# A decoder trunk on one core: the sparse-attention indexer summed pair by pair, and four loads moved between queues

## The chip, the cores and the metric

The kernel runs on one core of a Trainium2 chip. It is one launch; all weights are read from HBM once. The metric is the device time of that launch in microseconds (us). Times of single instructions and waits come from one profiled execution, whose own time stands beside the other runs below.

## What is computed

Two decoder layers on 512 tokens of width 1024, all in float32. Layer 0 mixes tokens with a gated linear recurrence (HGRN2), layer 1 with a sparse attention (DSA); each is followed by a SwiGLU feed-forward block with a causal convolution of width 3. Before each of the four blocks, and at the end, stands an RMS norm. The part that the change touches most is the indexer of layer 1, cut here to its core:

```python
proj = rms_norm(h, attn_norm[1]) @ w_in
q, k, v, q_idx, k_idx, w_idx = split(proj)      # q_idx: 8 heads of 64; k_idx: 64; w_idx: 8
dots   = einsum('bthd,bsd->bths', q_idx, k_idx)
scores = einsum('bths,bth->bts', relu(dots), w_idx * (8 ** -0.5 * 64 ** -0.5))
scores = where(key_pos <= q_pos, scores, -1e30)
sel    = top_k(scores, 128)                     # the keys that this query attends to
```

Attention then runs over the selected keys alone, here as a dense product with a mask: a key that was not selected gets a large penalty.

## The kernel before, in words

**Layout and engines.** Activations lie transposed, 128 features on the partitions by 512 tokens, in 8 blocks. Every float32 operand of a large product is split into a high and a low part (fp32r), and a product is three matmuls: high by high, high by low, low by high (`mm3`, L169 to L171). A weight tile of 128 x 1024 is loaded by `wunit` (L150, on SP's queue), and split on ACT (`whi`, L143) and on DVE or GpSimd (`wlo`, L144). Where `lo_engine` is None, `wlo` is made by ACT (L158) and an accumulating DMA of GpSimd's queue (L160), and `whi` by ACT at L159. There are three buffers of `whi` and of `wlo`: a new tile waits until the projection that read the buffer is finished. `proj_T` is one such projection: 24 matmuls into one PSUM bank `pj`.

**What sets the order.** TensorE's order is the program's own: `weave` runs a main generator and, by costs that each yields, lets side generators (`add_side`) put their matmuls between. The other engines' order is set by a scheduler when the kernel is built, and each runs its instructions in that order. So a matmul that stands early in TensorE's order and whose operand comes late holds up everything behind it.

**The third norm.** The sum of squares of layer 1's input (`sqa`, L215) goes through TensorE (`pq`, L240), DVE, and GpSimd (`rstd_c`, L248, four columns), and is turned back into rows by four transposes (`pr`, L252) and an ACT copy (`rstd_r`, L253). `norm_chain(wait)` yields `wait` before `pq`, and 4.2 before `pr`.

**The indexer.** `head_in` projects `k_idx` and `w_idx` first (72 columns, called pk here), then the eight heads of `q_idx` as four blocks of two heads, called b0 to b3. Of each block `stack` makes `qh` and `ql`: ACT copies the upper rows to `qh` (L675) and the lower to `ql` (L676), then DVE subtracts the residues into the other halves (L677, L678). `kw_evac` and `kw_weights` make `ki_h`, `ki_l` and the head weights `wN`. After all four blocks `dots` runs: for each of the query tiles t = 1, 2, 3 and for each block the two heads' products (`pi`, L749, widths 256, 384, 512), ReLU on ACT (L759, two buffers `relu`), and the weighted sum into `sc[t]` on DVE (L755, L760). Meanwhile TensorE goes on with the projections of K, V and q (`rest_in`), whose results DVE scales (`tmp`, L696).

**The selection.** `top` finds the 128 largest scores by 16 rounds of MAX (L774) and MATCH_REPLACE (L776) on DVE, first for t = 1 alone, then for t = 2 and 3 together, and writes the mask `sel` (L779). The attention units take `sel1` and later `sel2` and `sel3` as an operand of TensorE (L860), so TensorE waits there if DVE is late.

**Start.** The first instructions load `cols` (all norm gains and small vectors, 25 KB, ACT's queue), the conv constants `convc` (L117, ACT's queue), the first half of x in pieces (L413) and the first weights (L150), both on SP's queue. The first real matmul (L425) needs `whi` (L141), and x scaled by `cols` (L133).

Of the kernel before, what the change touches and what calls it, by code (L numbers as in the profile page):

```python
# [8 lines left out]
F32 = mybir.dt.float32  # L9
# [3 lines left out]
AF = mybir.ActivationFunctionType  # L13
ALU = mybir.AluOpType
# [3 lines left out]
P = 128  # L18
D = 1024
T = 512  # L20
# [3 lines left out]
NEG = -1e30  # L24
# [24 lines left out]
def trunk(ctx: ExitStack, tc: tile.TileContext, xT, vecs, convs, hgrn_w_in, hgrn_w_out, dsa_w_in, dsa_w_out,  # L49
          rel_bias, ffn_w_up, ffn_w_down, c_masks, c_onehot, out, dbg=None, stop=99):  # L50
    nc = tc.nc
# [9 lines left out]
    def bank(name):  # L61
        return ps.tile([P, 512], F32, name=name, tag="bank")
# [16 lines left out]
    nrm = ctx.enter_context(tc.tile_pool(name="nrm", bufs=2))  # L79

    cols = const.tile([P, 49], F32, name="cols")
    nc.scalar.dma_start(cols, vecs)
    gn_col = cols[:, 48:49]
    ident = const.tile([P, P], F32, name="ident")
    make_identity(nc, ident)
    convc = const.tile([P, 2, 4, 2 * FB], F32, name="convc")
# [12 lines left out]
    rstd_c = const.tile([P, TT], F32, name="rstd_c")  # L99
# [9 lines left out]
    def late_constants():  # L109
        yield 6.0  # L110
        raw = wraw.tile([P, 1024], F32, name="wr", tag="wr")
        mk = raw[:, :len(LEVELS) * P + 192]
        nc.scalar.dma_start(mk, c_masks)
        nc.vector.tensor_copy(masks, mk[:, 192:].rearrange("p (l t) -> p l t", t=P))
        for i in range(3):
            nc.vector.tensor_copy(pairs[:, i], mk[:, None, i * 64:i * 64 + 64].to_broadcast([P, TT, 64]))
        nc.scalar.dma_start(convc.rearrange("p l w b -> p (l w b)"), convs)  # L117
        nc.scalar.dma_start(far, bass.AP(tensor=rel_bias.tensor, offset=rel_bias.offset + (REL_BUCKETS - 1) * AH,
                                         ap=[[0, P], [1, AH]]))
        rb, oneh = raw[:REL_BUCKETS, 1000:1000 + AH], raw[:REL_BUCKETS, 576:576 + BAND]  # L120
        nc.scalar.dma_start(rb, rel_bias)
        nc.scalar.dma_start(oneh, c_onehot)
        yield 6.0
        pz = bank("pz")
        nc.tensor.matmul(pz[:AH, :BAND], rb, oneh, start=True, stop=True)
        bz = mk[:AH, :BAND]
        nc.vector.memset(bz, -NEG)
        nc.scalar.activation(bz[:, 127:383], pz[:AH, :256][:, ::-1], AF.Copy, scale=-1.0)
        nc.scalar.dma_start(Z, bz)
# [16 lines left out]
    def wunit(src, nk, n, first=False, dst=None):  # L146

        raw = wraw.tile([P, 1024], F32, name="wr", tag="wr")
        rv = raw[:, :nk * n].rearrange("p (k n) -> p k n", k=nk)
        nc.sync.dma_start(rv, src.rearrange("(k p) n -> p k n", p=P))  # L150
        if dst:
            hi, lo = (a.rearrange("p a b -> p (a b)") for a in dst)
        else:
            hi = wsp.tile([P, 1024], F32R, name="whi", tag="whi")
            lo = wsp.tile([P, 1024], F32R, name="wlo", tag="wlo")
        if lo_engine[0] is None and not dst:

            nc.scalar.activation(lo[:, :nk * n], raw[:, :nk * n], AF.Copy, scale=-1.0)  # L158
            nc.scalar.activation(hi[:, :nk * n], raw[:, :nk * n], AF.Copy)  # L159
            nc.gpsimd.dma_start(lo[:, :nk * n].rearrange("p (k n) -> p k n", k=nk),  # L160
                                src.rearrange("(k p) n -> p k n", p=P), accum_op=ALU.add)
        else:
            split(hi[:, :nk * n], lo[:, :nk * n], raw[:, :nk * n], lo_engine[0] or nc.vector,
                  nc.vector if first else None)
        return (hi[:, :nk * n].rearrange("p (k n) -> p k n", k=nk),
                lo[:, :nk * n].rearrange("p (k n) -> p k n", k=nk))
# [18 lines left out]
    side, done = [], set()  # L185

    def add_side(gen, rate=1.0):
        side.append([gen, rate, 0.0])
# [472 lines left out]
    with ExitStack() as sx:  # L661
        ds_ = sx.enter_context(tc.tile_pool(name="ds", bufs=1))
        bias = ds_.tile([P, AH, T], F32, name="bias")
        qh = ds_.tile([P, KB, T], F32R, name="qh")
        ql = ds_.tile([P, KB, T], F32R, name="ql")
# [5 lines left out]
        def stack(b, src, lo):  # L671

            a, c = qh[:, b, :], ql[:, b, :]
            top_, bot = rows2
            nc.scalar.activation(a[top_], src[top_], AF.Copy)  # L675
            nc.scalar.activation(c[bot], src[bot], AF.Copy)  # L676
            lo.tensor_tensor(a[bot], src[top_], a[top_].bitcast(F32), op=ALU.subtract)  # L677
            lo.tensor_tensor(c[top_], src[bot], c[bot].bitcast(F32), op=ALU.subtract)  # L678
# [4 lines left out]
        wN = ds_.tile([P, TT, 8], F32, name="wN")  # L683
        scs = ds_.tile([P, 9 * P], F32, name="scs")
        sc = [None, scs[:, 7 * P:], scs[:, 4 * P:7 * P], scs[:, :4 * P]]
        m8 = ds_.tile([P, TT, 8], F32, name="m8")

        with ExitStack() as sy:
            iy = sx.enter_context(tc.tile_pool(name="iy", bufs=1))
            ix = sy.enter_context(tc.tile_pool(name="ix", bufs=1))  # L690
            ki_h = ix.tile([P, T], F32R, name="ki_h")
            ki_l = ix.tile([P, T], F32R, name="ki_l")
# [16 lines left out]
            def kw_weights():  # L709
                tmp = kw.pop()  # L710
                pw = bank("pw")
                for t in range(TT):
                    nc.tensor.transpose(pw[:, t * 72:(t + 1) * 72], tmp[:72, t * P:(t + 1) * P], ident[:72, :72])
                for t in range(TT):
                    nc.vector.tensor_scalar(wN[:, t, :], pw[:, t * 72 + 64:(t + 1) * 72], 8 ** -0.5 * 64 ** -0.5,
                                            rstd_c[:, t:t + 1], op0=ALU.mult, op1=ALU.mult)

            def setup():

# [13 lines left out]
            def head_in():  # L733
                pk = yield from proj_T(w_in, O_KI, 72)
                for b in range(4):
                    o = yield from proj_T(w_in, O_QI + b * P,
                                          hook=({7: lambda: kw_evac(pk)}, {2: kw_weights}, None, None)[b])
                    lo_engine[0] = nc.gpsimd
                    stack(4 + b, o, nc.vector)

            def dots():
                for t in range(1, TT):
                    w = (t + 1) * P
                    ts_ = slice(t * P, (t + 1) * P)
                    for b in range(4):
                        o = [bank("pi") for _ in range(2)]
                        for k_ in (ki_h, ki_l):
                            for e in range(2):
                                nc.tensor.matmul(o[e][:, :w], (qh, ql)[e][:, 4 + b, ts_], k_[:, :w],  # L749
                                                 start=k_ is ki_h, stop=k_ is ki_l)  # L750
                        yield 0.22 * (t + 1)
                        for e in range(2):
                            i = 2 * b + e
                            if i == 0:
                                nc.vector.tensor_scalar(sc[t], o[e][:, :w], 0.0, wN[:, t, 0:1],  # L755
                                                        op0=ALU.max, op1=ALU.mult)
                            else:
                                r_ = ix.tile([P, T], F32, name="relu", bufs=2)
                                nc.scalar.activation(r_[:, :w], o[e][:, :w], AF.Relu)  # L759
                                nc.vector.scalar_tensor_tensor(sc[t], r_[:, :w], wN[:, t, i:i + 1], sc[t],  # L760
                                                               op0=ALU.mult, op1=ALU.add)
                    nc.gpsimd.affine_select(sc[t][:, w - P:], sc[t][:, w - P:], pattern=[[-1, P]], base=0,
                                            channel_multiplier=1, compare_op=ALU.is_ge, fill=NEG)
                    done.add(f"sc{t}")
                    if t == 1:
                        add_side(top((1,)), 0.4)

            def top(ts):

                while any(f"sc{t}" not in done for t in ts):  # L770
                    yield 0.5
                for r in range(16):
                    for t in ts:
                        nc.vector.max(m8[:, t, :], sc[t])  # L774
                    for t in ts:
                        nc.vector.match_replace(sc[t], m8[:, t, :], sc[t], -3e38)  # L776
                    yield sum(2 * (0.065 + (t + 1) * P / 960) for t in ts)
                for t in ts:
                    nc.vector.tensor_scalar(sel[t], sc[t], -2e38, -NEG, op0=ALU.is_gt, op1=ALU.mult)  # L779
                    done.add(f"sel{t}")  # L780
                if 3 not in ts:
                    add_side(top((2, 3)), 0.55)
# [26 lines left out]
                    done.add(f"q{b}")  # L809
                done.add("q8")  # L810

            add_side(norm_chain())
            add_side(setup())
            weave(head_in())
            add_side(dots(), 1.0)
            rest = rest_in()
            for c in rest:
                weave([c])
# [220 lines left out]
```

## Time and profile before

| | |
|---|---|
| three runs | 1273.42, 1273.68 (median), 1275.24 us |
| profiled execution: its own time | 1276.48 us |
| profiled execution: span of its instructions | 1274.7 us |
| busy in the span: TensorE (PE) | 1251.4 us (98%) |
| busy in the span: VectorE (DVE) | 803.0 us (63%) |
| busy in the span: ScalarE (ACT) | 599.6 us (47%) |
| busy in the span: GpSimd (POOL) | 138.8 us (11%) |
| DMA | 124.05 MB, mean 97 GB/s |

TensorE is busy almost throughout; the time outside the span is 1.8 us. The profiled execution is 2.8 us above the median of the three others. A busy PE counts a matmul from its start to a modelled end, so two that follow each other overlap; steps from start to start tell the pace.

### The profile page before, as it was taken

The numbers are of one execution on the slowest core, as the hardware profiler recorded it, in microseconds if no ns is written. First come the engines' busy times: TensorE is split into PE (matmuls) and PEld (weight loads), VectorE is DVE, ScalarE is ACT, GpSimd is POOL, SyncE is SP. The second block draws the span as 40 slices with busy tenths as digits, with TensorE's granted clock in tenths as the row PEclk, the third lists the DMA queues.
The fourth block names the chain that finished last, engine by engine and source line by source line (L and its number), as shares of the span: only waits on it lengthen the run. The fifth ranks groups of instructions, "written<-read, shape, count | busy, mean of one in ns | idle before, by whom it ended". The sixth has DMA issues, their size and how long they took to land.

```text
span 1274.7 us, 15695 instructions
## 1 busy us (share of the span) xinstructions
PE 1251.4 (98%) x6054; PEld 1046.2 (82%) x6054; DVE 803.0 (63%) x1305; ACT 599.6 (47%) x989; POOL 138.8 (11%) x120
## 2 busy tenths in 40 slices
PE   8999999999999999999999998999999999999997
PEld 7788888887888888888887777988888888888887
DVE  7755777756777777742444999635677777762331
ACT  5546565444544444421337757853444444441430
POOL 3022223110000000000003453300000000000000
PEclk9999999999999999999999999999999999999999
DMA  6339777323333333322237850003233333333222
GB/s 199 117 73 158 133 129 126 76 66 99 91 93 98 99 99 99 98 91 93 87 103 173 134 109 25 27 1 99 83 100 99 99 99 94 92 95 99 91 75 66
DMA packets 199178, 124.05 MB, mean 97 GB/s; under 512 B 5264, under 2 KB 188480, under 8 KB 199104
## 3 DMA queue, kind: packets, MB, share of 16 engines
q1 hardware_dynamic: 170320, 108.31, 28.7%
q0 software_dynamic: 28080, 14.16, 9.3%
q8 instruction: 47, 0.77, 0.3%
q10 hardware_dynamic: 704, 0.58, 0.2%
q14 instruction: 27, 0.22, 0.1%
HBM read 120.92 MB, written 2.12 MB: 97 GB/s over the span
## 4 chain that ended last, share of the span: by engine, by line
PE 88%; DVE 7%; ACT 2%; issue 1%; DMA 0%; POOL 0%; DVEq 0%; SPq 0%; POOLq 0%; ACTq 0%
PE pj L169 17%; PE pj L171 17%; PE pj L170 17%; PE px L169 9%; PE px L171 9%; PE px L170 9%; PE pav L923 2%; DVE scs L776 2%; PE pl L556 1%; PE po L602 1%; DVE m L774 1%; DVE scs L760 1%; PE pl L863 1%; PE pt L912 1%; PE pn L170 1%
## 5 line engine op out<-in xcount | busy, mean ns | idle before, releaser
L169 PE MATMUL pj<-x,whi 128*128 128x512 f32 (+1 forms) x1016 | 403.0, 397 | 0.0
L171 PE MATMUL pj<-x,wlo 128*128 128x512 f32 (+1 forms) x1016 | 396.9, 391 | 1.1 <-DMA wlo<-in_dsa_w_in_dram 1.1
L170 PE MATMUL pj<-x,whi 128*128 128x512 f32 (+1 forms) x1016 | 396.3, 390 | 0.0
L144 DVE TENSOR_TENSOR wlo<-wr,whi 128x1024 fp32r<-128x1024 f32 (+2 forms) x165 | 202.0, 1224 | 155.1 <-ACT whi L143 153.1
L143 ACT ACTIVATE whi<-wr 128x1024 fp32r<-128x1024 f32 (+1 forms) x167 | 173.6, 1039 | 257.1 <-PE px L170 155.2
L171 PEld LDWEIGHTS pj<-x,wlo 128*128 128x128 f32 (+1 forms) x1016 | 190.6, 188 | 42.4 <-DMA wlo<-in_dsa_w_in_dram 1.5
L169 PEld LDWEIGHTS pj<-x,whi 128*128 128x128 f32 (+1 forms) x1016 | 191.0, 188 | 39.2 <-issue 1.6
L170 PEld LDWEIGHTS pj<-x,whi 128*128 128x128 f32 (+1 forms) x1016 | 191.1, 188 | 38.8 <-issue 1.0
L169 PE MATMUL px<-ah,whi 128*128 128x512 f32 (+1 forms) x332 | 128.5, 387 | 0.0
L171 PE MATMUL px<-ah,wlo 128*128 128x512 f32 (+1 forms) x332 | 127.5, 384 | 0.0
L170 PE MATMUL px<-al,whi 128*128 128x512 f32 (+1 forms) x332 | 126.2, 380 | 0.0
L348 DVE TENSOR_TENSOR ub<-pj,rstd_r 128x512 f32<-128x512 f32 x88 | 60.6, 688 | 82.3 <-PE pj L171 77.3
L143 ACT ACTIVATE ah<-c 128x512 fp32r<-128x512 f32 x44 | 27.8, 631 | 115.9 <-DVE c L360 115.9
L171 PEld LDWEIGHTS px<-ah,wlo 128*128 128x128 f32 x332 | 62.3, 188 | 13.5
L170 PEld LDWEIGHTS px<-al,whi 128*128 128x128 f32 x332 | 62.3, 188 | 12.8
L351 ACT ACTIVATE c<-ub,convc 128x512 f32<-128x512 f32 x88 | 71.2, 809 | 2.4 <-DVE ub L348 1.6
L169 PEld LDWEIGHTS px<-ah,whi 128*128 128x128 f32 x332 | 62.4, 188 | 11.4
L353 DVE SCALAR_TENSOR_TENSOR c<-ub,convc,c 128x512 f32<-128x512 f32 x88 | 66.2, 752 | 3.0
L358 ACT ACTIVATE c<-c 128x512 f32<-128x512 f32 x44 | 27.8, 632 | 80.8 <-DVE c L353 80.7
L352 DVE SCALAR_TENSOR_TENSOR c<-ub,convc,c 128x512 f32<-128x512 f32 x88 | 65.6, 746 | 0.0
L522 DVE TENSOR_TENSOR qk<-qk,ftree 128x512 f32<-128x512 f32 x56 | 39.6, 709 | 17.6 <-PE pl L560 7.1
L144 DVE TENSOR_TENSOR al<-c,ah 128x512 fp32r<-128x512 f32 x44 | 30.4, 692 | 29.3 <-ACT ah L143 29.3
(226 smaller groups left out, 1743.9 us busy)
## 6 DMA issues: line engine op xcount, KB each, us to landing
wr<-in_ffn_w_up_dram SPq DMA_DIRECT2D x88, 512.0 KB, 3.8
wr<-in_ffn_w_down_dram SPq DMA_DIRECT2D x41, 512.0 KB, 3.7
wr<-in_hgrn_w_in_dram SPq DMA_DIRECT2D x30, 512.0 KB, 4.1
wlo<-in_hgrn_w_in_dram POOLq DMA_DIRECT2D x19, 512.0 KB, 7.5
wr<-in_dsa_w_in_dram SPq DMA_DIRECT2D x14, 512.0 KB, 3.7
wr<-in_hgrn_w_out_dram SPq DMA_DIRECT2D x8, 512.0 KB, 3.6
wlo<-in_dsa_w_in_dram POOLq DMA_DIRECT2D x8, 512.0 KB, 7.8
wr<-in_dsa_w_out_dram SPq DMA_DIRECT2D x8, 512.0 KB, 3.8
```

The costliest lines, as they stand in the source:

```text
L143: nc.scalar.activation(dst_h, src, AF.Copy)
L144: lo.tensor_tensor(dst_l, src, dst_h.bitcast(F32), op=ALU.subtract)
L169: nc.tensor.matmul(o, ah, bh, start=start, stop=False)
L170: nc.tensor.matmul(o, ah, bl, start=False, stop=False)
L171: nc.tensor.matmul(o, al, bh, start=False, stop=stop)
L348: nc.vector.tensor_tensor(u[:, 2:], o, rows(), op=ALU.mult)
L351: nc.scalar.activation(c, u[:, 2:], AF.Identity, scale=cc[2], bias=cc[3])
L352: nc.vector.scalar_tensor_tensor(c, u[:, 1:T + 1], cc[1], c, op0=ALU.mult, op1=ALU.add)
L353: nc.vector.scalar_tensor_tensor(c, u[:, 0:T], cc[0], c, op0=ALU.mult, op1=ALU.add)
L358: nc.scalar.activation(g, g, AF.Silu)
L522: nc.vector.tensor_tensor(turned(m), turned(m), factors(ft, m), op=ALU.mult)
L776: nc.vector.match_replace(sc[t], m8[:, t, :], sc[t], -3e38)
```

## The change

Four edits.

1. `dots()` over all four blocks, added after the four projections, becomes `dots(b)`, added as soon as block b is stacked. Inside it the loops are turned round: for each block, all three query tiles. It waits in the program's order until `wN` is written. The mask of the diagonal and `top` follow after the last block.
2. `norm_chain(4.8)` in place of the default 3.6 for the third norm: `pq` stands later in TensorE's order.
3. `cols` is loaded by GpSimd's queue instead of ACT's; the first weight tile by ACT's queue instead of SP's.
4. The load of `convc` is held back: a one-column ACT copy from `rstd_c` into `convc` is put ahead of it, so that it starts after the first norm.

The diff, cut to its core:

```diff
-    nc.scalar.dma_start(cols, vecs)
+    nc.gpsimd.dma_start(cols, vecs)
...
+
+        nc.scalar.activation(convc[:, 0, 0, 0:1], rstd_c[:, 0:1], AF.Copy)
         nc.scalar.dma_start(convc.rearrange("p l w b -> p (l w b)"), convs)
...
-        nc.sync.dma_start(rv, src.rearrange("(k p) n -> p k n", p=P))
+        (nc.scalar if first else nc.sync).dma_start(rv, src.rearrange("(k p) n -> p k n", p=P))
...
+                done.add("wN")
...
                     stack(4 + b, o, nc.vector)
-
-            def dots():
+                    add_side(dots(b))
+
+            def dots(b):
+
+                while "wN" not in done:
+                    yield 0.3
                 for t in range(1, TT):
                     w = (t + 1) * P
                     ts_ = slice(t * P, (t + 1) * P)
-                    for b in range(4):
-                        o = [bank("pi") for _ in range(2)]
...
+                    o = [bank("pi") for _ in range(2)]
+                    for k_ in (ki_h, ki_l):
                         for e in range(2):
...
+                    if b == 3:
+                        nc.gpsimd.affine_select(sc[t][:, w - P:], sc[t][:, w - P:], pattern=[[-1, P]], base=0,
...
-            add_side(norm_chain())
+            add_side(norm_chain(4.8))
             add_side(setup())
             weave(head_in())
-            add_side(dots(), 1.0)
```

TensorE (PE), where the indexer's products stand. Before, they begin after block b3 (`pj_5223`) and one step of the K projection (`pj_5259`), with the products of b0 for two heads:

```order
L169 MATMUL pj_5223<-x_79,whi_5219 128x512
L170 MATMUL pj_5223<-x_81,whi_5219 128x512
L171 MATMUL pj_5223<-x_79,wlo_5220 128x512
L169 MATMUL pj_5259<-x_78,whi_5254 128x512
L170 MATMUL pj_5259<-x_80,whi_5254 128x512
L171 MATMUL pj_5259<-x_78,wlo_5255 128x512
L749 MATMUL pi_5263<-ki_h_5032,qh_5012 128x256
L749 MATMUL pi_5264<-ki_h_5032,ql_5013 128x256
L749 MATMUL pi_5263<-ki_l_5033,qh_5012 128x256
L749 MATMUL pi_5264<-ki_l_5033,ql_5013 128x256
```

In the changed kernel, the end of block b1 (`pj_5137`) and what follows it:

```order
L171 MATMUL pj_5137<-x_79,whi_5133 128x512
L172 MATMUL pj_5137<-x_81,whi_5133 128x512
L173 MATMUL pj_5137<-x_79,wlo_5134 128x512
L171 MATMUL pj_5215<-x_78,whi_5211 128x512
L172 MATMUL pj_5215<-x_80,whi_5211 128x512
L173 MATMUL pj_5215<-x_78,wlo_5212 128x512
L755 MATMUL pi_5223<-ki_h_5033,qh_5013 128x256
L755 MATMUL pi_5224<-ki_h_5033,ql_5014 128x256
L755 MATMUL pi_5223<-ki_l_5034,qh_5013 128x256
L755 MATMUL pi_5224<-ki_l_5034,ql_5014 128x256
L755 MATMUL pi_5235<-ki_h_5033,qh_5013 128x384
L755 MATMUL pi_5236<-ki_h_5033,ql_5014 128x384
```

The products of b1 now stand three matmuls after b1's own projection; those of b2 and b3 stand in the same way behind theirs, and those of b0 three matmuls behind the transposes `pw`, in the middle of b1. After the second width another step of three matmuls and the 512 wide products follow.

ScalarE (ACT) at the same place, before: the blocks' copies (`qh`, `ql` from `pj`), each after a weight tile `whi` and ahead of the next tile's `wlo`, with no `relu` until b3 is done:

```order
L159 ACTIVATE whi_5254<-wr_5252 128x1024
L675 ACTIVATE qh_5012<-pj_5136 64x512
L676 ACTIVATE ql_5013<-pj_5136 64x512
L158 ACTIVATE wlo_5255<-wr_5252 128x1024
L159 ACTIVATE whi_5394<-wr_5392 128x1024
L675 ACTIVATE qh_5012<-pj_5184 64x512
L676 ACTIVATE ql_5013<-pj_5184 64x512
```

and in the changed kernel:

```order
L161 ACTIVATE whi_5357<-wr_5355 128x1024
L677 ACTIVATE qh_5013<-pj_5137 64x512
L678 ACTIVATE ql_5014<-pj_5137 64x512
L160 ACTIVATE wlo_5358<-wr_5355 128x1024
L765 ACTIVATE relu_5229<-pi_5223 128x256
L765 ACTIVATE relu_5232<-pi_5224 128x256
L765 ACTIVATE relu_5244<-pi_5235 128x384
L765 ACTIVATE relu_5247<-pi_5236 128x384
L765 ACTIVATE relu_5262<-pi_5250 128x512
L765 ACTIVATE relu_5265<-pi_5251 128x512
L161 ACTIVATE whi_5440<-wr_5438 128x1024
```

The order of `whi`, `qh`, `ql`, `wlo` is kept; six `relu` of the block come in behind it. On DVE the two subtractions of a block and then its six additions into `sc` follow in the same way.

GpSimd (POOL) at the third norm, before, where the `wlo` are those of b1, b2, b3:

```order
L722 MEMSET vf_5018 128x1536
L144 TENSOR_TENSOR wlo_5133<-wr_5130,whi_5132 128x1024
L248 TENSOR_TENSOR rstd_c_110<-ms_5062,half_97 128x4
L144 TENSOR_TENSOR wlo_5181<-wr_5178,whi_5180 128x1024
L144 TENSOR_TENSOR wlo_5220<-wr_5217,whi_5219 128x1024
```

and in the changed kernel:

```order
L725 MEMSET vf_5019 128x1536
L146 TENSOR_TENSOR wlo_5134<-wr_5131,whi_5133 128x1024
L146 TENSOR_TENSOR wlo_5212<-wr_5209,whi_5211 128x1024
L250 TENSOR_TENSOR rstd_c_110<-ms_5069,half_97 128x4
L146 TENSOR_TENSOR wlo_5287<-wr_5284,whi_5286 128x1024
```

`rstd_c` has moved behind a second weight tile. In TensorE's order `pq` stands six matmuls later and `pr` 18 matmuls behind it where it stood 21.

## Rows read from the trace of the kernel before

**Rows 1.** Busy time by stretch: PE, PEld, DVE, ACT, POOL, granted clock, DMA, GB/s.

```profile
720.00:740.00 20.00, 18.30 (x83) 14.59 (x82) 20.00 (x61) 12.65 (x17) 10.63 (x9) 1.00 0.92 158
...
743.70:747.20 3.50, 3.50 (x11) 2.72 (x10) 2.82 (x12) 1.97 (x8) 0.07 (x1) 0.51 0.90 111
...
790.00:800.00 10.00, 9.44 (x66) 8.53 (x65) 9.48 (x30) 7.91 (x24) 5.49 (x4) 1.00 0.36 110
```

**Rows 2.** PE's waits, 668 to 800: total us, times, longest.

```profile
PE pl L860 <- DVE sel L779: 3.9, 2, 2.1
PE pav L923 <- ACT px L916: 1.8, 3, 0.8
PE pj L171 <- DMA wlo<-in_dsa_w_in_dram: 1.1, 1, 1.1
PE pq L240 <- DVE sqa L215: 0.9, 1, 0.9
PE pt L796 <- DVE tmp L696: 0.6, 1, 0.6
```

**Rows 3.** Timeline of PE: start, duration, operation, idle time before and its releaser.

```profile
683.97 0.48 PE L169 MATMUL pj<-x,whi 128*128 128x512 f32 x1
...
687.50 0.39 PE L169 MATMUL pj<-x,whi 128*128 128x512 f32 x1
...
698.38 0.39 PE L169 MATMUL pj<-x,whi 128*128 128x512 f32 x1
...
742.62 0.38 PE L860 MATMUL pl<-sel,identb 128*128 128x256 bf16 x2 [2.14 <-DVE sel L779]
...
743.79 0.63 PE L171 MATMUL pj<-x,wlo 128*128 128x512 f32 x1
...
747.18 0.40 PE L170 MATMUL pj<-x,whi 128*128 128x512 f32 x1
...
788.71 0.50 PE L860 MATMUL pl<-sel,identb 128*128 128x384 bf16 x2 [1.77 <-DVE sel L779]
```

**Rows 4.** Timeline of ACT around the end of b1.

```profile
687.53 1.06 ACT L159 ACTIVATE whi<-wr 128x1024 fp32r<-128x1024 f32 x1 [1.93 <-issue]
...
689.22 0.59 ACT L676 ACTIVATE ql<-pj 64x512 fp32r<-64x512 f32 x1
```

**Rows 5.** Timeline of DVE: the last step of stacking b0 and b1.

```profile
688.06 0.69 DVE L678 TENSOR_TENSOR ql<-pj,ql 64x512 fp32r<-64x512 f32 x1
...
690.56 0.69 DVE L678 TENSOR_TENSOR ql<-pj,ql 64x512 fp32r<-64x512 f32 x1
```

**Rows 6.** Selection rounds on DVE, 742.6 to 789: count, busy us, mean ns.

```profile
L776 DVE MATCH_REPLACE8 scs<-m,scs 128x384 f32<-128x384 f32 (+1 forms) x24 | 14.5, 609 | 0.0
L774 DVE MAX8 m<-scs 128x8 f32<-128x512 f32 (+1 forms) x23 | 13.4, 616 | 0.0
```

**Rows 7.** Third norm: timelines of POOL, then of PE and ACT.

```profile
676.35 1.01 POOL L248 TENSOR_TENSOR rstd_c<-ms,half 128x4 f32<-128x4 f32 x1 [4.13 <-DVE ms L247]
677.33 2.39 POOL L144 TENSOR_TENSOR wlo<-wr,whi 128x1024 fp32r<-128x1024 f32 x1
...
679.19 0.60 PE L252 MATMUL pr<-ident,rstd_c 128*128 128x128 f32 x4
...
681.69 0.58 ACT L253 ACTIVATE rstd_r<-pr 128x512 f32<-128x512 f32 x1
```

**Rows 8.** Start: timeline of all engines.

```profile
3.91 0.17 DVE L400 TENSOR_TENSOR lb_e<-cols 128x8 f32<-128x8 f32 x1 [2.88 <-DMA cols<-in_vecs_dram]
...
5.78 0.43 DVE L141 CAST whi<-wr 128x512 fp32r<-128x512 f32 x1 [0.61 <-DMA wr<-in_hgrn_w_in_dram]
...
6.35 0.77 PE L425 MATMUL pn<-whi,x 128*128 128x512 f32 x1 [1.48 <-DVE whi L141]
```

**Rows 9.** DMA issues: count, KB each, median us from issue to landing.

```profile
wr<-in_dsa_w_in_dram SPq DMA_DIRECT2D x14, 512.0 KB, 3.7
wlo<-in_dsa_w_in_dram POOLq DMA_DIRECT2D x8, 512.0 KB, 7.8
```

More of the change, by code (lines that the diff above doesn't have):

```diff
@@ L744, in dots @@
                     ts_ = slice(t * P, (t + 1) * P)
-                    for b in range(4):
-                        o = [bank("pi") for _ in range(2)]
[L747 to L751, printed above, removed]
-                        for e in range(2):
[L753 to L766, printed above, removed]
+                    o = [bank("pi") for _ in range(2)]
+                    for k_ in (ki_h, ki_l):
+                        for e in range(2):
+                            nc.tensor.matmul(o[e][:, :w], (qh, ql)[e][:, 4 + b, ts_], k_[:, :w],
+                                             start=k_ is ki_h, stop=k_ is ki_l)
@@ new lines, in dots @@
+                    yield 0.22 * (t + 1)
+                    for e in range(2):
+                        i = 2 * b + e
+                        if i == 0:
+                            nc.vector.tensor_scalar(sc[t], o[e][:, :w], 0.0, wN[:, t, 0:1],
+                                                    op0=ALU.max, op1=ALU.mult)
+                        else:
+                            r_ = ix.tile([P, T], F32, name="relu", bufs=2)
+                            nc.scalar.activation(r_[:, :w], o[e][:, :w], AF.Relu)
+                            nc.vector.scalar_tensor_tensor(sc[t], r_[:, :w], wN[:, t, i:i + 1], sc[t],
+                                                           op0=ALU.mult, op1=ALU.add)
@@ L768, in top @@
+                    if b == 3:
+                        nc.gpsimd.affine_select(sc[t][:, w - P:], sc[t][:, w - P:], pattern=[[-1, P]], base=0,
+                                                channel_multiplier=1, compare_op=ALU.is_ge, fill=NEG)
+                        done.add(f"sc{t}")
+                        if t == 1:
+                            add_side(top((1,)), 0.4)
             def top(ts):
```

## The prediction

> **What bounds the kernel now.** I read the busy time by stretch first, then TensorE's waits, then the timelines of the engines that it waits for. TensorE (PE) is the bound in most of the program, so only what makes it wait, or run slower, is worth anything. Around the attention of layer 1 it is not: from 720 to 740 us DVE is busy for all 20.00 us and PE for 18.30 [rows 1]. Between 668 and 800 us PE waits 3.9 us for the selection masks in two waits, 1.8 us for attention weights from ACT, 1.1 us for a weight transfer, 0.9 us for the sum of the third norm and 0.6 us for a DVE scaling [rows 2]: 8.3 us in all. One wait costs more than itself. After the 2.14 us wait at 742.62 the granted clock was 0.51, the 1.2 GHz level, for about 3.5 us [rows 1, 3]: eight matmuls took from 743.79 to 747.18, 3.39 us. At the full clock one step is (698.38 - 687.50) / 48 = 0.227 us [rows 3], eight are 1.82, so the stretch lost 1.6 us. After the 1.77 us wait at 788.71 the clock stayed at 1.00 [rows 1, 3].
>
> **The indexer pair by pair: new waits on PE.** Nothing is added or removed; 48 matmuls, 21 ReLUs and 24 DVE operations move. What counts is when their operands come. In PE's new order the products of a block stand three matmuls behind the end of its projection, and the second of them needs `ql`, the last thing that stacking the block makes.
>
> How long does stacking take? In the trace of before nobody waits for it, so it can be read undisturbed. Block b1's last matmul gives way to b2's first at 687.50 [rows 3]. At 687.53 ACT begins a weight tile, which was held up until b1 released its buffer, for 1.06 us; then come `qh` and `ql`, the latter from 689.22 to 689.81 [rows 4]; then two DVE subtractions, the last from 690.56 to 691.25 [rows 5]. So `ql` is ready 3.75 us after the block's end. PE comes to the product that reads it after three steps of 0.227 and one of half that width, 0.80 us: at 688.30. The wait is 691.25 - 688.30 = 2.95 us. ACT's order of weight tile, `qh`, `ql` is the same behind b1, b2 and b3, and it is the same in the new program, so I take it three times: 8.9 us. For b0 the new place is three matmuls behind the transposes: 683.97 + 0.7 + 0.1 = 684.8 [rows 3], and b0's `ql` is ready at 688.06 + 0.69 = 688.75 [rows 5]: 3.9 us. Together 12.8 us. The bounds: 9 us, if each wait were shorter by 1 us because the weight tile were out of the way, and 14 us, if DVE's or ACT's moved ReLUs and additions get in ahead; they stand behind in the order, so I take 12.8. Queued behind each waiting product on PE is the rest of the next block, and so everything after it.
>
> **The clock behind these waits.** Each new wait is at least as long as the one that was followed by half clock (2.14 us) and longer than the one that was not (1.77 us). A single product with `qh` alone runs 0.7 us before the end of each. One case on either side doesn't say which of four will be followed by such a stretch; the bounds are none and four, 0 to 6.3 us at 1.57 each. I take three: 4.7 us.
>
> **What comes back.** PE now arrives at the later waits some 11 us later than before, while DVE has done 18 of its 24 additions during the blocks. At best the mask waits (3.9 us) go, with them the 1.6 us of half clock, the transfer's wait (1.1: its issue stood behind ReLUs on ACT that are now done) and the scaling's (0.6): 7.2 us. The waits for attention weights (1.8) stay: both ends of them move together. The other bound is that the masks stay late, since the first scores of t = 1 are now complete only after the last block, and only 1.7 us come back. I take 7.2, because DVE has less left to do at the same point of PE's order.
>
> **The third norm.** Six matmuls more stand ahead of `pq`, 6 x 0.227 = 1.4 us, which covers the wait of 0.9 us [rows 2]. But GpSimd now makes a weight tile ahead of `rstd_c`: 2.39 us and then 1.01 [rows 7]. That tile could start at about 676.4, when `rstd_c` started before, so `rstd_c` is ready at about 676.4 + 2.4 + 1.0 = 679.8. PE comes to `pr` three matmuls later and 0.9 us earlier than before: 679.19 + 0.7 - 0.9 = 679.0 [rows 7]. It waits 0.8 us there. Net 0, between -0.9 and +0.7. What is late next: the copy `rstd_r` starts on ACT only at 681.69 [rows 7], after the new end of `pr` (679.8 + 0.6), so b0's stacking doesn't move.
>
> **The start.** Before, DVE idles 0.61 us for the first weights, and PE's first product follows at 6.35 [rows 8]. First on ACT's queue instead of second on SP's, they can come at most those 0.6 us earlier. Four small operations on DVE (0.17 us each, as the one at 3.91 [rows 8]) now stand behind the first tile instead of ahead: 0.7 us later for what follows. `cols` on GpSimd's queue is not shown by any row; before it landed at 3.91 [rows 8] and was not last. The nearest rows for the queue are 7.8 us from issue to landing for GpSimd's accumulating 512 KB, 3.7 for SP's [rows 9], so 0 to 4.1 us later; being 25 KB without accumulation it is nearer to 0. At 8.0 it would delay PE's start by some 3 us. I take 0 for the start, from -0.6 to +3.
> The Trainium skill speaks against this edit: DMA: Bandwidth & Descriptors, section "Issuing engine by pattern", gives simple loads to the sync engine's queue and calls GpSimd's software path generally slower, with first bytes after about 1 us against 0.6 in its Specifications. By that page, as an estimate, `cols` would land 0.4 us later, at 4.3, still ahead of the weights, and the sum would not move; no row of before shows such a load.
>
> **The conv constants.** One small ACT copy (at most the 0.58 us of the 512 wide `rstd_r` copy [rows 7]) and one load move behind the first norm; their first use is in the feed-forward block, long after. 0 us; if that cover were gone, one small transfer.
>
> **The sum.** 12.8 + 4.7 - 7.2 + 0 + 0 = +10.3 us. The profiled execution would go from 1276.48 to 1286.8; the median of the runs stands 2.8 us below it, and against that median, 1273.68, I predict 1284.0 us.
>
> **The rivals.**
> *No half clock.* The waits come, but at most one of them is followed by a slow stretch, as the 1.77 us wait was: 12.8 - 7.2 + 0 to 1.6 = +5.6 to +7.2, about 1280. For it: only one case of four or five longer waits in the trace lost clock. Against: that one was the shortest of what I expect here. Chance 0.22.
> *The selection becomes the bound.* With t = 1 complete only after the last block, the rounds start over 10 us later. A round of t = 2 and 3 is two MAX and two MATCH_REPLACE, 2 x (0.616 + 0.609) = 2.45 us [rows 6]; two rounds short on arrival cost 4.9 us on top of the forecast: 1289. For it: DVE had no idle time before. Against: the additions moved away from that stretch. Chance 0.12.
> *Everything returns.* The waits are 12.8, no slow stretch follows, all 9.0 us (with the 1.8) come back and the start gains 0.6: +3.2; a further 1 us anywhere makes it no change, 1276. Chance 0.10.
> *The pair is there in time* (faster). If stacking finished within the 0.8 us that PE takes to arrive, none of the four waits would exist and the 7.2 to 9.0 us would be gain: 1265 to 1266.5. It decides in favour of the change as soon as the four waits together are under about 7 us, 1.8 each. Against it: 3.75 us read directly. Chance 0.06.
> *The norm edit doesn't do what it says* is in the sum: its wait moves from `pq` to `pr`.
>
> **How the numbers follow.** The forecast has 0.50 and, with two to four slow stretches and a mask wait of up to 2 us, its own range is 1281 to 1288. The range that should hold 8 in 10 takes in most of the first rival and part of the second: 1277 to 1289. A measurement of this kernel can tell about 0.2%, 2.5 us, from no change, so slower is above 1276.2: forecast and first two rivals, 0.84; the third is the same, 0.10; the fourth faster, 0.06.
>
> **What would show it.** In the profile of the changed kernel: four waits of PE at the first or second `pi` of width 256, released by DVE's `ql` subtraction, 3 to 4 us each with the lone product between; stretches at half clock behind most; the waits for `sel` shorter; `pq` without a wait and `pr` with one of about 0.8 us. The prediction is wrong if these products run without waiting, if the clock holds through them, or if the masks are still waited for by 2 us and more.

## The result and the profile after

The changed kernel takes 1293.99 us (median of 1296.93, 1293.17, 1294.82 and 1291.28), the kernel before 1273.68 beside it: 1.0157 times as long, 95% interval 1.0133 to 1.0182. The forecast was 1284.0, the range 1277 to 1289: slower, as predicted, but by 20.3 us in place of 10.3. The profiled execution is the slowest of the four, 1296.93 us with a span of 1295.0. Lines of the new kernel are those of before plus 2 at the start, plus 6 or 7 from the indexer's products on.

TensorE's waits between 668 and 830 us, to be held against [rows 2] (engine, line and tile that wait, what they wait for, us in total, times, longest):

```profile
PE pi L755 <- DVE qh L679: 9.6, 4, 3.3
PE pl L866 <- DVE sel L786: 2.1, 1, 2.1
PE pav L929 <- ACT px L922: 1.9, 2, 1.0
PE pi L755 <- DVE ql L680: 1.5, 4, 0.4
PE pt L921 <- DVE rs L897: 1.0, 1, 1.0
PE pr L254 <- POOL rstd_c L250: 1.0, 1, 1.0
```

The four new waits at `pi` are there, 11.1 us. One of the two waits for masks is still there, with its full 2.1 us. The waits for the later masks, for a weight transfer, for `tmp` and for `pq` are gone; two new ones of 1.0 each have come (`rs`, `pr`).

One of the four places, TensorE's timeline behind block b1 (start, duration, engine, line, operation, in brackets the wait ahead):

```profile
699.96 0.39 PE L173 MATMUL pj<-x,wlo 128*128 128x512 f32 x1
702.44 0.38 PE L755 MATMUL pi<-ki_h,qh 128*128 128x256 f32 x1 [2.09 <-DVE qh L679]
703.26 0.36 PE L755 MATMUL pi<-ki_h,ql 128*128 128x256 f32 x1 [0.43 <-DVE ql L680]
...
704.39 0.63 PE L171 MATMUL pj<-x,whi 128*128 128x512 f32 x1
704.82 0.63 PE L172 MATMUL pj<-x,whi 128*128 128x512 f32 x1
```

From the last matmul to the first product 2.48 us pass where a step takes 0.227, and from the first to the second product 0.82 where about 0.2 would do: 2.87 us lost. From 704.39 on the matmuls follow each other at 0.43 us, no longer at 0.227. Why it waits stands on ACT and DVE:

```profile
699.53 1.06 ACT L161 ACTIVATE whi<-wr 128x1024 fp32r<-128x1024 f32 x1 [1.30 <-PE pj L172]
700.49 0.57 ACT L677 ACTIVATE qh<-pj 64x512 fp32r<-64x512 f32 x1
701.08 0.59 ACT L678 ACTIVATE ql<-pj 64x512 fp32r<-64x512 f32 x1
```

```profile
701.71 0.68 DVE L679 TENSOR_TENSOR qh<-pj,qh 64x512 fp32r<-64x512 f32 x1 [2.69 <-ACT ql L678]
702.42 0.69 DVE L680 TENSOR_TENSOR ql<-pj,ql 64x512 fp32r<-64x512 f32 x1
```

This is the sequence of [rows 4, 5]: a weight tile first, then two copies, then two subtractions, the last of which ends at 703.11.

The windows of the granted clock (us from : to, length, busy time and instructions of PE, PE's loads, DVE, ACT and POOL, then the granted clock). In this execution all four waits, and the one for the first mask, are followed by 3.41 us at 0.50, the 1.2 GHz level:

```profile
690.00:694.12 4.12, 1.37 (x8) 1.20 (x9) 3.72 (x9) 0.35 (x1) 0.00 (x0) 1.00 0.47 127
694.12:697.53 3.41, 3.41 (x10) 2.73 (x9) 1.97 (x5) 0.53 (x2) 0.00 (x0) 0.50 0.00 0
...
704.36:707.77 3.41, 3.41 (x10) 2.67 (x9) 2.03 (x4) 1.63 (x5) 0.60 (x1) 0.50 1.06 202
...
714.60:718.01 3.41, 3.18 (x10) 2.81 (x11) 1.73 (x4) 1.59 (x5) 1.55 (x1) 0.50 0.62 160
...
728.25:731.66 3.41, 3.41 (x10) 2.74 (x9) 2.85 (x7) 1.58 (x4) 1.16 (x3) 0.50 1.07 202
...
762.38:765.80 3.42, 3.42 (x11) 2.84 (x11) 3.42 (x16) 3.39 (x9) 2.46 (x2) 0.50 1.15 179
```

The start, DVE and then TensorE, against [rows 8]:

```profile
7.67 0.17 DVE L402 TENSOR_TENSOR lb_e<-cols 128x8 f32<-128x8 f32 x1 [6.64 <-DMA cols<-in_vecs_dram]
...
8.21 0.69 DVE L146 TENSOR_TENSOR wlo<-wr,whi 128x512 fp32r<-128x512 f32 x1
```

```profile
8.75 1.65 PE L427 MATMUL pn<-whi,x 128*128 128x512 f32 x3 [3.93 <-ACT x L135]
```

`cols` comes at 7.67, not at 3.91, and is now what everything waits for. The first product starts 2.4 us later, and the clock is 0.50 from 8.04 to 14.86, where the profile of before has 1.00.

### The profile page after: what moved, and what is told of

The parts are those of the page before. It is cut to its first block, busy times and chain, and to the rows that moved or that the text cites. A ratio compares the mean times of both kernels' runs of the same rounds, so it can differ in the third digit from the quotient of the medians.

```text
span 1295.0 us, 15694 instructions
## 1 busy us (share of the span) xinstructions
PE 1261.1 (97%) x6054; PEld 1053.9 (81%) x6054; DVE 804.5 (62%) x1305; ACT 599.5 (46%) x990; POOL 136.3 (11%) x121
## 5 line engine op out<-in xcount | busy, mean ns | idle before, releaser
L172 PEld LDWEIGHTS px<-al,whi 128*128 128x128 f32 x332 | 62.4, 188 | 12.7
```

The source lines that it names most:

```text
L172: nc.tensor.matmul(o, ah, bl, start=False, stop=False)
```

## The experiments

Each ran beside the kernel before on the same chip; the base is the median of before in that session. A difference in us is against that base.

| kernel | base | median | ratio, 95% interval |
|---|---|---|---|
| e1_pairs | 1274.02 | 1287.88 | 1.0115 (1.0089 to 1.0141) |
| e2_norm | 1274.02 | 1273.75 | 1.0000 (0.9991 to 1.0010) |
| e3_cols | 1274.02 | 1276.76 | 1.0018 (1.0009 to 1.0027) |
| e4_wts_conv | 1274.02 | 1278.30 | 1.0026 (1.0015 to 1.0037) |
| e5_wts | 1273.76 | 1278.04 | 1.0034 (1.0021 to 1.0046) |
| e6_late | 1273.76 | 1273.54 | 0.9991 (0.9981 to 1.0001) |
| e7_late_sel | 1273.76 | 1277.19 | 1.0027 (1.0016 to 1.0038) |
| e8_fill | 1273.76 | 1283.98 | 1.0081 (1.0066 to 1.0096) |
| e9_order | 1274.81 | 1276.60 | 1.0015 (1.0004 to 1.0026) |
| e10_hold | 1274.81 | 1275.37 | 1.0010 (0.9997 to 1.0023) |
| e11_before_hold | 1274.81 | 1277.72 | 1.0022 (1.0013 to 1.0031) |
| e12_hold_norm | 1274.81 | 1275.56 | 1.0002 (0.9992 to 1.0012) |
| e13_mix | 1274.99 | 1273.52 | 0.9989 (0.9980 to 0.9999) |
| e14_mix_lo | 1274.99 | 1272.04 | 0.9976 (0.9965 to 0.9987) |
| e15_late_lo | 1274.99 | 1274.11 | 0.9991 (0.9982 to 1.0001) |

### Which edit costs what

Of the loads, two change queue (`cols` and the first weight tile) and a third, `convc`, is held back on its own queue. Four kernels carry one part of the change each, on the kernel before: e1_pairs the whole `dots(b)` edit, e2_norm `norm_chain(4.8)`, e3_cols the first change below, e4_wts_conv the other two.

```diff
-    nc.scalar.dma_start(cols, vecs)
+    nc.gpsimd.dma_start(cols, vecs)
...
-        nc.sync.dma_start(rv, src.rearrange("(k p) n -> p k n", p=P))
+        (nc.scalar if first else nc.sync).dma_start(rv, src.rearrange("(k p) n -> p k n", p=P))
...
+        nc.scalar.activation(convc[:, 0, 0, 0:1], rstd_c[:, 0:1], AF.Copy)
         nc.scalar.dma_start(convc.rearrange("p l w b -> p (l w b)"), convs)
```

> Only the indexer edit (pair by pair); start and third norm as in the kernel before. Theory A (the parts add up, and this one carries most of the loss): four waits of TensorE at the pi products, 12.7 us together, each followed by a stretch at half clock, less what comes back later (some 4 us: the second and third mask, one weight transfer): 1287 to 1291 us. Theory B (the half clock behind the waits came with the later start, whose slow stretch was longer too): the same four waits, at most one slow stretch behind them: 1282 to 1284 us.

> Only the third norm's later sum. Theory A: the wait at pq (0.9 us) goes and one at pr of about the same length comes: within 0.7 us of 1273.7. Theory B (the wait at pr in the changed kernel comes from the indexer's other DVE and GpSimd order): pq's wait goes and none comes, 1272.8 us.

> Only the vectors (cols) by GpSimd's queue. Theory A: this queue alone makes them land late, near 7.7 us instead of 3.9, and the first real product starts 2.4 us later: 1276.1 us. Theory B: in the changed kernel they were late because three queues with other contents stood beside them; alone they land by 5 us and nothing moves: 1273.7 us.

> Only the first weights by ACT's queue and the conv constants later; cols by ACT's queue as before. Theory A: the first weights land 0 to 0.6 us earlier, 1273.1 to 1273.7 us. Theory B: the first weights on ACT's queue stand behind cols there and come later than on SP's, up to 2.4 us: 1276 us.

Measured: +13.9, -0.3, +2.7 and +4.3 us. The parts add up to 20.6 where the whole change costs 20.3, and the pairs carry two thirds. e1_pairs is theory A: its profile has the four waits (10.8 us) and half clock (0.50, the 1.2 GHz level) behind three of them. e2_norm is theory A: the wait moves from `pq` to `pr` (0.9 us each). e3_cols is theory A: the queue alone makes `cols` late. Its timeline has the issue, and then the first instruction that reads them:

```profile
1.29 0.77 POOL L82 DMA_DIRECT2D cols<-in_vecs_dram  x1 [0.84 <-POOLq L1029]
...
6.87 0.17 DVE L400 TENSOR_TENSOR lb_e<-cols 128x8 f32<-128x8 f32 x1 [5.83 <-DMA cols<-in_vecs_dram]
```

From issue to use 5.6 us, where ACT's queue took 3.2 (0.74 to 3.91, [rows 8]), and the issue itself stands 0.55 us later. e4_wts_conv is slower than either theory's reason allows for: theory A had nothing, B had 2.4. Its ten runs fall in two groups by the clock: four from 1275.4 to 1276.3 at 0.997 or 0.998, six from 1278.3 to 1279.5 at 0.994. The median lies in the upper group; the mean of the ten is 3.4 above the mean of the base.

### The first weights

e5_wts has only the middle change of the diff above; e9_order is e5_wts with one column copied, so that DVE makes the first low weight tile before the second block's low part:

```diff
+            wl0 = wl if k0 == 0 else wl0
...
+                    if k == 1:
+                        nc.vector.tensor_copy(xl[:, 1, 0:1], wl0[:, 0, 0:1])
                     split_gain(0, k)
```

> Of the start, only the first weights by ACT's queue; cols by ACT's queue, conv constants early. Theory A (the first weights' queue makes the loss of e4_wts_conv): 1278 us, with most runs some 3 us above the others by the clock. Theory B (the held back conv load makes it): 1274 us.

> First weights by ACT's queue as in e5_wts, and a copy of one column that makes DVE do the first low weight tile ahead of the second block's low part. Theory A (the queue itself costs nothing; with it DVE's order changed, the low tile then fell together with GpSimd's first addition, took 1.76 us in place of 0.68, and TensorE waited 1.7 us for it, the half clock behind): the tile is ready near 7.5 us, 1274 to 1275 us. Theory B (the weights themselves come later on ACT's queue): 1278 us.

e5_wts is +4.3 as e4_wts_conv: the held back conv load costs nothing that can be measured, as predicted, and the weights' queue is the loss. Yet TensorE's first product is no later: 6.39 against 6.35 [rows 8]. What is late is the next operand. The low weight tile on DVE in the kernel before:

```profile
6.79 0.68 DVE L144 TENSOR_TENSOR wlo<-wr,whi 128x512 fp32r<-128x512 f32 x1
```

e5_wts, TensorE, DVE and GpSimd:

```profile
6.39 1.24 PE L425 MATMUL pn<-whi,x 128*128 128x512 f32 x4 [1.89 <-DVE whi L141]
9.28 0.79 PE L425 MATMUL pn<-wlo,x 128*128 128x512 f32 x1 [1.66 <-DVE wlo L144]
```

```profile
6.80 0.75 DVE L134 SCALAR_TENSOR_TENSOR x<-hT,cols,x 128x512 fp32r<-128x512 f32 x1 [0.56 <-ACT x L133]
7.47 1.76 DVE L144 TENSOR_TENSOR wlo<-wr,whi 128x512 fp32r<-128x512 f32 x1
```

```profile
7.37 1.30 POOL L215 TENSOR_TENSOR sqa<-sqa,sq 128x512 f32<-128x512 f32 x1 [6.06 <-ACT sq L214]
```

With the weights on another queue the scheduler laid DVE's work out in another order. The low weight tile now stands behind an instruction that waits for ACT, then falls together with an addition of GpSimd and takes 1.76 us in place of 0.68: it ends 0.56 us after GpSimd's addition does. The Trainium skill, "SBUF — State Buffer", section "SBUF: two separate sides", states that two such operations share a pair of ports, and that the one that starts later is kept out until the earlier one is done; the trace agrees: GpSimd's addition starts first, at 7.37, and ends at 8.67, and 8.67 + 0.56 = 9.23 us is the end of the tile. In e9_order the tile comes first again, on DVE:

```profile
6.47 0.69 DVE L144 TENSOR_TENSOR wlo<-wr,whi 128x512 fp32r<-128x512 f32 x1
```

TensorE has no wait there (`pn<-wlo` at 7.71), and the profiled execution of e9_order takes 1275.01 us, as theory A has it; but its ten runs lie between 1274.0 and 1279.0 with a median 1.8 above its base. So DVE's order makes 2.5 of the 4.3 us.

The clock is part of it. In e5_wts it is at 0.50 for 6.82 us, around the wait for the late tile:

```profile
7.33:14.15 6.82, 5.16 (x13) 3.80 (x13) 6.82 (x7) 5.08 (x9) 4.65 (x3) 0.50 0.77 259
```

In e9_order it is so from 7.43 to 10.85 alone, and in the profile of before not at all. What causes the other 1.8 us is not shown. The profiles hint at something other than the queue: e4_wts_conv and e5_wts have one more stretch at half clock, 1.6 us lost, behind the wait for the first mask at 745 us, as the profile of before has; e2_norm, e3_cols and e9_order have the same wait of 2.1 us without it. How many of the other executions have it is not on record.

### Half clock, or the waits alone

e8_fill is e1_pairs with twelve products of ones where TensorE stood still:

```diff
+                    if t == 1:
+                        for _ in range(12):
+                            nc.tensor.matmul(o[0], ones_r, ones_r[:, None, :].to_broadcast([P, 4, P]), start=True, stop=True)
```

> As e1_pairs, with twelve products of ones (2.7 us) ahead of each pair's first product, into the bank that this product overwrites: TensorE works where it stood still. Theory A (the half clock behind the four waits comes from TensorE standing still): no half clock from 680 to 735 us and three stretches of 1.57 us less, 1283 us. Theory B (the clock falls there for another reason, or the filling only adds to the waits): 1288 us or, with 2.7 us on top of each wait, up to 1298 us.

1283.98 us, 3.9 below e1_pairs (3.6 if each is taken against its own base), though nothing else was taken away: theory A. The products of ones take up the waits and no more: behind b2 the second product starts 3.30 us after the block's last matmul in both (703.71 to 707.01 in e1_pairs, 702.31 to 705.61 in e8_fill). The same stretch of both kernels, e1_pairs first (the column behind POOL's is the granted clock):

```profile
680.00:735.00 55.00, 44.14 (x181) 35.59 (x180) 34.29 (x72) 28.25 (x47) 12.16 (x10) 0.91 0.50 88
```

```profile
680.00:735.00 55.00, 54.52 (x251) 44.54 (x250) 38.40 (x84) 31.29 (x50) 13.75 (x11) 1.00 0.55 98
```

So the half clock behind the four waits was worth 3.9 us in the median run, between two and three stretches of 1.57; the 10.2 us that e8_fill stands above its base are the filled time, less what comes back later.

### Without the waits, and still no gain

e6_late starts each pair's products 4 to 5 us behind the end of its block, when stacking is done. e7_late_sel writes the rounds closer together besides.

```diff
             def dots(b):
 
+                yield 6.0 if b == 0 else 3.9
                 while "wN" not in done:
```

> Pair by pair, but each pair's products begin 4 to 5 us behind the end of its block instead of 0.7 us; all else as before. Theory A (the loss of the pairs is the 3.75 us that stacking takes, waited for four times, and nothing else in the idea is bad): no waits at pi, all scores complete near 706 us where before the last were at 725, the mask waits go with the half clock behind the first: 1274.0 - 3.9 - 1.6 = 1268 us, with the transfer's 1.1 also back 1267. Theory B (DVE sets the masks' time whatever the order): no waits at pi, but the masks are waited for as before: 1273 to 1275 us.

> As e6_late, and the selection rounds stand closer in the program's order (0.6 and 0.65 in place of 0.4 and 0.55 per unit of TensorE's work). Theory A (with the scores early the masks are no longer waited for): as e6_late within 1 us. Theory B (the masks' waits remain in e6_late because of the order written for the rounds): 2 to 4 us below e6_late.

No wait at `pi` is left in either, and the 13.9 us of e1_pairs are gone: the stacking time was the whole loss. But e6_late is only level with before: theory B. Its waits:

```profile
PE pav L929 <- ACT px L922: 2.3, 2, 1.9
PE pl L866 <- DVE sel L786: 1.9, 1, 1.9
PE pj L172 <- ACT wlo L159: 1.5, 1, 1.5
PE pq L241 <- DVE sqa L216: 0.9, 1, 0.9
```

The last scores are complete at 717.1 us, where before needed until 724.8; the later masks come at 783.5, where before had them at 788.3; but the first comes at 743.91, where before had it at 741.83. DVE was busy for all of 720 to 740 us and ran the rounds of t = 2 and 3 in between those of t = 1. e7_late_sel was 3.7 us worse than e6_late, against both theories: its attention units stood almost a block earlier in TensorE's order, and TensorE waited 6.4 us there for a mask that came at 743.6.

### Order or load on DVE

e10_hold lets the rounds of t = 2 and 3 begin only when the first mask is written; e11_before_hold does that to the kernel before; e12_hold_norm is e10_hold with the third norm's steps at 4.8 and 5.6; e13_mix lets them begin when half of the first rounds are done; e14_mix_lo is e13_mix with DVE relieved of the last two q blocks' weight tiles, and e15_late_lo is e6_late with that alone. The first piece below is in e10_hold, e11_before_hold and e12_hold_norm, the second in e13_mix and e14_mix_lo, the third in e14_mix_lo and e15_late_lo:

```diff
+                if 3 in ts:
+                    for t in ts:
+                        nc.vector.tensor_copy(m8[:, t, :], sel[1][:, :8])
...
+                    if ts == (1,) and r == 7:
+                        nc.vector.tensor_copy(m8[:, 2:4, :], m8[:, 1:2, :].to_broadcast([P, 2, 8]))
...
-                    lo_engine[0] = nc.vector if b >= 6 else None
+                    lo_engine[0] = None
```

> As e6_late, and the rounds of t = 2 and 3 wait until the mask of t = 1 is written (two copies of eight columns from it). Theory A (in e6_late the first mask was late, at 743.9, because its rounds shared DVE with those of t = 2 and 3): the first mask stands near 731 us, its wait goes with the half clock, 1273.5 - 1.9 - 1.6 = 1270 us or less. Theory B (the later masks then come later by as much and are waited for, and for the units behind them ACT): 1273.5 us.

> The kernel before with only the hold of e10_hold. Theory A (the pairs' earlier scores are needed for the gain): the first mask's wait of 2.1 us becomes smaller, but the masks of t = 2 and 3, waited for by 1.8 us already, come no earlier: 1271 to 1273 us. Theory B (the hold alone is the gain): as e10_hold.

> As e10_hold, and both steps of the third norm later (the sum at 4.8, the transposes 5.6 behind it in place of 4.2). Theory A (neither is then waited for, and the copy behind them is not needed earlier): 0.9 us below e10_hold. Theory B (the later row copy delays the first block's stacking or the head weights): as e10_hold or above it.

> As e6_late, with the rounds of t = 2 and 3 held until half of the rounds of t = 1 are done. Theory A (order: there is one in which neither mask is waited for): first mask near 739, last near 785, the first's wait of 1.9 us goes, with the half clock behind it: 1270 us. Theory B (DVE has too much to do there in all): one of the masks is still waited for, by 2 us or more, 1273 to 1275 us.

> As e13_mix, and the last weight tiles of the projections are made by ACT and GpSimd's accumulating transfer instead of DVE (1.2 us each on DVE). Theory A: as e13_mix. Theory B: DVE is done 2.4 us or more earlier, and the time is 2 to 3 us below e13_mix.

> As e6_late, with the last weight tiles off DVE as in e14_mix_lo, but no hold. Theory A (order): the first mask stays late (the tiles are made after it), 1273.5 us. Theory B (load): masks and units behind them come 2 us earlier, 1271 us.

DVE's timelines, the masks alone: e10_hold, e13_mix, e14_mix_lo, e15_late_lo.

```profile
733.28 0.29 DVE L789 TENSOR_SCALAR sel<-scs 128x256 bf16<-128x256 f32 x1
...
789.19 0.69 DVE L789 TENSOR_SCALAR sel<-scs 128x384 bf16<-128x384 f32 x2
```

```profile
739.44 0.30 DVE L788 TENSOR_SCALAR sel<-scs 128x256 bf16<-128x256 f32 x1
784.92 0.69 DVE L788 TENSOR_SCALAR sel<-scs 128x384 bf16<-128x384 f32 x2
```

```profile
739.19 0.47 DVE L788 TENSOR_SCALAR sel<-scs 128x256 bf16<-128x256 f32 x1
...
780.78 0.42 DVE L788 TENSOR_SCALAR sel<-scs 128x512 bf16<-128x512 f32 x1
```

```profile
744.33 0.27 DVE L786 TENSOR_SCALAR sel<-scs 128x256 bf16<-128x256 f32 x1
...
778.40 0.42 DVE L786 TENSOR_SCALAR sel<-scs 128x512 bf16<-128x512 f32 x1
```

Holding all the later rounds brings the first mask 10.6 us forward and the last some 6 back: TensorE's wait of 1.9 for the first becomes one of 4.0 for the later ones, and the time is level with its base: theory B of e10_hold. On the kernel before the same hold costs 2.9 us, against both theories there. In e12_hold_norm neither `pq` nor `pr` is waited for, but `pw` is, by 0.9 us: theory B again, the wait went one step further down the chain.

Half the hold (e13_mix) leaves a wait of 2.6 for the later masks, 1.5 us below its base: theory B. Relief alone (e15_late_lo) leaves 2.1 for the first, though the last mask comes 5 us earlier than in e6_late; its time can't be told from its base: theory A. Both together leave no wait for a mask, and e14_mix_lo takes 1272.04 us: 3.0 us below before, 22 below the changed kernel, 1.5 below e13_mix (theory B, which had 2 to 3). By its median it is the best version of the study; single runs of e6_late, which lie from 1269.85 to 1275.30, reach lower. TensorE now waits 3.3 us there for ACT's attention weights (`pav`), where before it waited 1.8. So the masks were late for both reasons, the order of the rounds and DVE's load. Relief is not the whole of its gain; each of the two alone is worth 1.5 us or less.

## What the prediction had right, and which steps failed

**The waits at `pi`: right.** 12.8 us were worked out; from start to start the new places lose 4.08, 2.87, 2.88 and 2.88, together 12.7 us. The 3.75 us of stacking, read where nobody waited for it, was the right number, and so was the choice to leave ACT's weight tile ahead of it. Only the split was another: most of each wait, 2.1 to 3.3 us, is ahead of the first product, since `qh` too is complete only with a DVE subtraction, and 0.2 to 0.4 is left ahead of the second.

**The clock behind them: right in size.** 4.7 us were taken, three stretches; e8_fill measures 3.9. The profile of the changed kernel has one behind all four waits, 6.3 us, that of e1_pairs behind three. How many a run has was open in the prediction and is open still.

**What comes back: the first step that failed.** Of the two bounds, 7.2 and 1.7 us, 7.2 were taken "because DVE has less left to do at the same point of PE's order". The wait for the later masks (1.8), the transfer's (1.1) and the scaling's (0.6) did go, 3.5 us, but the first mask's wait stayed with 2.1 and its half clock, and `rs` brought 1.0. Net 2.5, a miss of 4.7 us. (The 1.6 us of half clock were not safe to count in any case: they were read in an execution 2.8 us above the median to which the sum was then applied, and the profile of e2_norm, 1273.83 us, has the same wait for the first mask with the clock at 1.00 from 720 to 760 us.) The reason argued from the number of additions done, and passed over which ones: with the blocks in the outer loop, every score is complete only after b3, and DVE idles while stacking is waited for. The busy time of all engines from 690 to 725 us (the last line of the windows), before and after:

```profile
sum 35.00, PE 34.30 PEld 28.65 DVE 26.73 ACT 25.56 POOL 11.57; mean PE 8.58 PEld 7.16 DVE 6.68 ACT 6.39 POOL 2.89
```

```profile
sum 35.00, PE 26.68 PEld 21.14 DVE 17.05 ACT 14.75 POOL 3.15; mean PE 6.67 PEld 5.28 DVE 4.26 ACT 3.69 POOL 0.79
```

DVE does 9.7 us less there, and 11.1 less if the stretch is taken 4.7 us later in the changed kernel (694.74 to 729.74, 15.67 us), by as much as TensorE is behind at `pr`. The scores of t = 1 masked by GpSimd, and the first mask on DVE, in the kernel before:

```profile
706.70 0.29 POOL L762 TENSOR_SCALAR_AFFINE_SELECT scs<-scs 128x128 f32<-128x128 f32 x1 [2.26 <-DVE scs L760]
...
741.83 0.73 DVE L779 TENSOR_SCALAR sel<-scs 128x256 bf16<-128x256 f32 x1
```

and in the changed kernel, with the product of TensorE that waits for it:

```profile
729.28 0.29 POOL L769 TENSOR_SCALAR_AFFINE_SELECT scs<-scs 128x128 f32<-128x128 f32 x1 [0.46 <-DVE scs L766]
...
761.46 0.48 DVE L786 TENSOR_SCALAR sel<-scs 128x256 bf16<-128x256 f32 x1
...
761.99 0.38 PE L866 MATMUL pl<-sel,identb 128*128 128x256 bf16 x2 [2.13 <-DVE sel L786]
```

The scores of t = 1 are masked 22.6 us later, 4.7 of them from before the indexer. From there DVE does need less for the first mask, 32.2 us in place of 35.1. But TensorE comes sooner too, 30.6 us after the scores in place of 33.8, since in its order all products of t = 2 and 3 but the last four are done by then. The first mask comes 19.6 us later and TensorE's wait for it begins 19.4 us later, so the wait was kept. The prediction named this as its other bound (1.7 us) and, in part, as a rival, "the selection becomes the bound", and gave both too little. That the rival's price of 4.9 us is near the miss of 4.7 is luck: it stood for two rounds short, and what was missed is the wait of 2.1, the 1.6 behind it and the 1.0 of `rs`. With 2.5 in place of 7.2 the pairs come to 12.7 + 3.9 - 2.5 = 14.1; e1_pairs measured 13.9.

**The third norm: right.** `pq` no longer waits, `pr` waits 0.95 against 0.8 worked out, and e2_norm is level with before.

**The start: the second step that failed.** 0 us were taken, with a range up to +3. By the medians the runs give 2.7 for `cols` and 4.3 for the weights, 7.0 together; the whole change less e1_pairs leaves 6.4 (20.3 - 13.9). Two reasons were wrong. For `cols` the size of 25 KB was taken to speak for the low end of 0 to 4.1 us; it came 3.0 us later in e3_cols and 3.8 in the changed kernel, near the upper bound, though the prediction had worked out itself that 8.0 would cost some 3 us. The estimate from the Trainium skill, "DMA: Bandwidth & Descriptors", section "Specifications", was 0.4 us later: the direction, against the edit, holds here, the size does not. For the weights "at most those 0.6 us earlier" was a bound on one side only: that moving a load changes the order in which DVE works, and so what it collides with, was not looked for. In the changed kernel itself the low tile comes early again (8.21, 0.69 us), so that there the two losses are not the same two, and that the medians add up is partly luck.

TensorE's sum of the first norm (`pq`) tells how far the start alone reaches. It begins at 36.2 us in the changed kernel, at 31.6 to 33.9 with a mean of 33.0 in the twelve profiles of kernels whose start is that of before, at 35.0 in e3_cols and 35.3 in e5_wts. So 3.2 of the 6.4 us are lost by then. The rest comes later, and in the profiles it is half clock: the changed kernel has a stretch from 247.0 to 250.4, 1.6 us lost behind a wait of 1.5 that before has too (two of the twelve profiles with the old start have one there), and behind b3 and the first mask two stretches that e1_pairs does not have. That the start causes any of these three is not shown.

**The conv constants: right.** e4_wts_conv and e5_wts, which differ by them alone, differ by nothing that can be measured.

With the terms as the experiments measure them the sum is 12.7 + 3.9 - 2.5 + 2.7 + 4.3 = 21.1; the change costs 20.3. The prediction's own sign of being wrong, "the masks are still waited for by 2 us and more", is what the trace shows.

## What to carry to other kernels

Before a product is moved next to the operand it reads, read how long that operand takes in the trace of before: less the little that TensorE still has to do ahead of the product, it is waited for in full, and here the clock behind the wait added about a third. What is to come back later depends on when the *last* input of the late step is complete, not on how many have been worked off, and on how much sooner the engine that waits arrives as well; turning a loop round can move both the wrong way. And an edit to a load is also an edit to the order in which a scheduler lays out the engines that use it: compare that order at the place, not only the queue.

## What the runs showed of the hardware

- A 25 KB load took 5.6 to 6.4 us from GpSimd's issue to its first use at the start of the program, and 3.2 by ACT's queue.
- A wait of 2.1 to 3.3 us of TensorE was followed by 3.41 us at the 1.2 GHz level in some executions and places and not in others: of the four at `pi`, three in e1_pairs and four in the changed kernel; the wait of 2.1 us for the first mask in before and e5_wts, but not in e2_norm and e3_cols; one of 1.5 us near 244 us in three of the seventeen profiles. Keeping TensorE on useless products through the waits kept the clock at 1.00 and gave back 3.9 us.
- A DVE subtraction with two operands took 1.76 us in place of 0.68 beside a GpSimd addition and ended 0.56 us after it.
